# A hybrid mixer block on one core: the output gates' stage in the rounds' pools, and longer transfer estimates for the planner

## The chip, the cores and the metric

The program runs on one core of one Trainium2 chip. A core has a tensor engine (PE, whose weight loads are shown apart as PEld), a vector engine (DVE), a scalar engine (ACT), GpSimd (POOL), and SyncE (SP), which issues every transfer of this program from one queue. The metric is the device time of one execution in microseconds.

## The reference, cut to what matters

One layer over 256 context tokens and 2048 latent tokens of width 1024, in float32. A modulated norm and one wide input projection `z` come first; its columns go to four mixers, each with four heads and a forward and a backward scan over chunks of 64 tokens. The sum of the two scans is normalised by head and multiplied by an output gate that is also a part of `z`. An output projection, a squared-ReLU MLP and a last norm follow.

```python
z = (jnp.concatenate([hc, hx], axis=1) @ w_in[layer]).astype(jnp.float32)
z_ml, z_rw, z_gl, z_gd = _split(z, (ML_W, RW_W, GL_W, GD_W))
mixed = jnp.concatenate([_mlstm_mixer(z_ml, ...), _rwkv_mixer(z_rw, ...), _gla_mixer(z_gl, ...), _gdn_mixer(z_gd, ...)], -1)
x = x + gate1_x * (mixed[:, n_ctx:] @ w_out[layer])
x = x + gate2_x * _mlp(_rms(x, norm2_w[layer]) * (1 + scale2_x) + shift2_x, mlp_w1[layer], mlp_w2[layer])
return _rms(x, final_norm_w)
# in a mixer:
y_fwd = scan_fn(*fwd_args)
y_bwd = scan_fn(*[_rev(t, n_ctx) for t in bwd_args])
y = _head_rms(y_fwd + _rev(y_bwd, n_ctx), norm_w) * jax.nn.sigmoid(o)          # mLSTM; GLA and GDN gate with silu
# in the RWKV-7 and GDN scans, for each chunk:
sol = lax.linalg.triangular_solve(m, rhs, left_side=True, lower=True, unit_diagonal=True)
```

## The kernel before

The 36 chunks of 64 tokens are worked through in six parts (`CHUNKS`), in five **rounds** (round 0 takes the context and one latent part, the rounds 1 to 4 one part each). Each round normalises its tokens (`make_h`: POOL multiplies `xh` by the row norm `rbr`, ACT scales it and rounds it to `hh`, DVE leaves the rest in `hl`), multiplies them with the columns of `w_in` (PE tiles `ps_z`, each operand as a rounded part and a rest, so three products for one), and stores what the scans need in DRAM (`x_fm`, `x_tm`, `x_rows`, `x_bg`). `hh` and `hl` are one buffer each, so a round's first `ps_z` waits for the last `ps_z` of the round before.

Beside the projections run two streams that mostly wait for each other and for transfers:

- **Solves** (`solve`): the triangular systems of up to four units (a direction and two chunks). For each unit `solve_prep` loads `s_s_b` and `s_s_x`, makes products `ps_n` and stores a matrix to `x_sN`; `find` loads them together into `s_s_b`, inverts 32x32 blocks in 31 steps of two instructions (`s_t`, `s_s_x`; on POOL for the rounds 0 to 3, on DVE for round 4) and stores `x_sX`; then `solve_post` loads that for each unit, makes products `ps_s` and stores `x_t`. The tiles `s_s_b` and `s_s_x` have one buffer each, so units follow one another.
- **Groups** (`group`): one chunk of one direction. It loads `ff`, `kc`, `rw`, `t` and `tm`, makes products `ps_att`, `ps_ml`, `ps_R`, `ps_U` and `ps_S`, writes the next state `St`, and makes the outputs `ps_ym` and `ps_ylgr`, which are left in `yall`. The first of a chunk's two directions stores `yall` to `x_gat`; the **second** loads what the first left (the 512 columns `yp`) and the gates (640 columns `gat`), adds, runs `finish` (norm by head, gates on POOL), transposes (`ps_yT`) and stores to `x_mix`.

After round 4 comes the stage of the **output gates** (`out_gates`, called four times): `make_h` again, then for each of three column pairs `tm_tiles` multiplies (two `ps_z` tiles a pair) and a gate tile is put together in a `t4` tile and stored to `x_gat`. Sixteen groups run beside it. The **tail** then works on four blocks of 512 tokens: output projection (`ps_o`), MLP (`ps_f`, `ps_a`), last norm, with the other 24 groups beside it.

Memory is held in **pools**: `phase_pools` opens a set for a stage, and a tile of a new stage waits for the tiles of the old one whose memory it takes. In a pool a tag has a number of buffers; an allocation beyond it waits for the oldest to be read for the last time. The rounds share one set, prefix "r", the gate stage has a set "g", the tail a set "t".

The code is written as generators that `interleave` steps through. The order that the chip sees is made afterwards by a **planner** in the framework (`schedule_with_timeline_sim=True`): it simulates the program with a table of costs and writes out, for each engine, a list in the order in which its simulation started things. On the chip each engine runs its list in that order and waits where an input isn't there. A transfer's estimated length in this table thus decides how much other work the planner lists before the transfer's first reader.

Of the kernel before, what the change touches and what calls it, by code (L numbers as in the profile page):

```python
# [4 lines left out]

# [5 lines left out]

F32 = mybir.dt.float32
F32R = mybir.dt.float32r
# [37 lines left out]
GC = 1  # L51
# [124 lines left out]
class Kern:  # L176
# [1262 lines left out]
    def wt(self, nm, shape, bufs=None):  # L1439
        return self.wp.tile([128] + shape, F32, tag=nm, name=nm, bufs=bufs or 2)  # L1440

    def by_half(self, t, src):

        for h, p in enumerate(SL):
            self.dma(t[p], src[:, h])

    def group(self, d, c0):
        X, R, sl = self.X, range, SL
# [49 lines left out]
        for ft in R(2):  # L1498
            x, n = (2 * ft, 2) if hasq else (1 + ft, 1)
# [89 lines left out]
        new = self.state[d] = self.state_tile()  # L1589
# [11 lines left out]

        yall = self.lt("yall", [GC, 4, 128])
        if second:
            gat = self.lt("gat", [GC, 1152])
            self.by_half(gat[:, 0], X["gat"][c0])
            yp, gat = gat[:, :, 0:512].rearrange("p c (m f) -> p c m f", m=4), gat[:, :, 512:]
        for ms in ("m", "lgr"):
            b = self.bank(self.qa, "yy", "ps_y" + ms, 1)
            first, then, last = [], [], []
            for mi, mm in enumerate(ms):  # L1610
                w = 65 if mm == "m" else 64
                for ft, p in fp:
                    y = slice(128 * mi + w * ft, 128 * mi + w * ft + w)
                    f, c, t, v = {"m": (Lq[:, 2 + ft], cm(ft), Lt[:, 6 + ft], vm(ft)), "l": (ff[:, 4 + ft], cl(ft), lS[:, ft], vl(ft)),
                                  "g": (Lq[:, ft], f2[ft], Lt[:, 4 + ft], U[:, g2[ft]]),
                                  "r": (ff[:, 3 * ft], cr(ft), Lt[:, 3 * ft], vr(ft))}[mm]
# [21 lines left out]
        if not second:  # L1638
            for h, p in enumerate(sl):
                self.dma(X["gat"][c0, :, h, 0:512], yw[p, 0])  # L1640
        else:
            self.finish(yall, gat)
            b = self.psum("ps_yT", "yt" if "yt" in self.pb else "pp")
            for m in R(4):
                self.tr(b[:, 128 * m:128 * m + 128], yall[:, 0, m])
            yT = self.lt("sq", [512])
            self.act(yT, b, AF.Copy)
            self.dma(X["mix"][:, c0].rearrange("p m r t -> p (m r t)"), yT)
            self.done.add(c0)

    def finish(self, yall, gat):

        nh = 8 * GC
        bc = [128, nh, 64]
        sq = self.lt("sq", [512]).rearrange("p (n d) -> p n d", d=64)
        ss, rs = self.wt("ss", [nh]), self.wt("rs", [nh])
        y = yall.rearrange("p c m (f d) -> p (c m f) d", f=2)
        v = lambda t: t.rearrange("p (c m f) -> p c m f", c=GC, m=4)

        s1 = self.wt("s1", [GC, 2])  # L1660
        yr = yall[:, :, 3].rearrange("p c (f d) -> p c f d", f=2)
        self.V.reduce_sum(s1, yr, axis=AX.X)
        self.stt(yr, s1.unsqueeze(3).to_broadcast([128, GC, 2, 64]), -1.0 / 64, yr, ALU.mult, ALU.add)
        self.act(sq, y, AF.Square)
        self.V.reduce_sum(ss, sq, axis=AX.X)

        self.ts(v(ss)[:, :, 3], v(ss)[:, :, 3], 64 * (GN_EPS - EPS), ALU.add)
        self.ts(ss, ss, 1.0 / 64, ALU.mult, EPS, ALU.add)
        self.inv_sqrt(rs, ss, self.wt("rqt", [nh]))
        self.tt(y, y, rs.unsqueeze(2).to_broadcast(bc), ALU.mult)  # L1670
        self.tt(yall[:, :, 0:3], yall[:, :, 0:3], gat[:, :, 0:384].rearrange("p c (m f) -> p c m f", m=3), ALU.mult, e=self.G)
        gr = gat[:, :, 384:640].rearrange("p c (f x d) -> p c f x d", f=2, x=2)
        self.tt(yr, yr, gr[:, :, :, 0], ALU.mult, e=self.G)
        self.tt(yr, yr, gr[:, :, :, 1], ALU.add, e=self.G)
# [137 lines left out]
def body(ctx, tc, A, out):  # L1812
    K = Kern(ctx, tc, A, out)
# [7 lines left out]
    def groups(d, cs):  # L1821
        return [lambda c=c: K.group(d, c) for c in cs]
    down = lambda a, b: range(a, b - 1, -1)
    def mix(a, b):

        n = max(len(a), len(b))
        o = []
        for i in range(n):
            o += a[len(a) * i // n:len(a) * (i + 1) // n] + b[len(b) * i // n:len(b) * (i + 1) // n]
        return o  # L1830
# [13 lines left out]
    with ExitStack() as both:  # L1844
        K.sp = both.enter_context(tc.tile_pool(name="sp", bufs=1))
        with ExitStack() as es:
# [8 lines left out]
            c = [(0, K.cond(0, "s_b", 1))]  # L1855
# [17 lines left out]
                solves([(B, 24), (F, 18), (B, 22), (F, 20)], [(B, 20), (F, 22), (B, 18), (F, 24)], [(B, 6), (B, 4)], beside=True)  # L1873
                finals((F, 2), (F, 1), (B, 3))
            interleave(K.round_(4, r4), q, groups(F, range(10, 18)), 29, 0.1)
        with ExitStack() as es:
            K.phase_pools(es, "g", {"": 4, "gat": 2, "yall": 2, "sq": 1}, {"pp": 2, "pc": 1})
            gap = mix(groups(F, range(18, 24)), groups(B, down(25, 16)))
            interleave(chain(K.out_gates(5, 1), K.out_gates(4), K.out_gates(3), K.out_gates(2)), q, gap, 24, 0.1)
    with ExitStack() as es:  # L1880
        K.tail_pools(es)
        blocks = [[(16, 8)], [(8, 8)], [(24, 8)], [(4, 4), (32, 4)]]
        interleave(K.tails(blocks), q, mix(groups(B, down(15, 8)), groups(F, range(24, 32)))
                   + mix(groups(B, down(7, 4)), groups(F, range(32, 36))), 296, 0.0, 0.35)


# [13 lines left out]
```

## Time and profile before

| | us |
|---|---|
| median of the runs | 4298.56 (4298.08 to 4305.28, 3 runs) |
| the profiled execution, its own time | 4309.05 |
| its span | 4307.2 |
| PE busy in the span | 3517.9 (82%) |
| DVE / ACT / POOL busy | 2464.7 / 1399.0 / 1451.0 |
| rounds 0 to 4, about | 0 to 1970 |
| output gates' stage, about | 1970 to 2380 |
| tail, about | 2380 to 4307 |

The stages are told apart by their tiles: the first `gate` tile is written at 1989.3 and the last at 2357.4; the groups' last transfer of `gat` is issued at 3212.3. In a window's row the busy time of each engine stands with its instruction count, then the granted clock of PE as a share of full speed, the mean busy share of the DMA engines and their rate. A row of a list of waits reads: who waited, on which line, for whom, microseconds in total, times, the longest. In a timeline row the brackets hold the idle time just before and what ended it. Lines L184, L188, L192, L197, L200, L228 and L239 are helpers (`tt`, `ts`, `stt`, `act`, `dma`, `weave`, `mm`), so tiles tell more than lines.

### The profile page before, as it was taken

The page shows a single profiled execution, that of the slowest core. Times are in us where ns is not written, and L with a number is a line of the kernel's source. Part 1 is how long each engine was busy: PE and PEld are TensorE (multiplying, and loading weights), DVE is VectorE, ACT ScalarE, POOL GpSimd, SP SyncE. Part 2 cuts the span into 40 slices and gives each one's busy share as a digit, 9 for nine tenths or more (in the row PEclk, how much of TensorE's full clock was granted, in tenths as well). Part 3 has the DMA queues.
Part 4 walks back from the last instruction along what each step waited for, and adds up shares of the span by engine and source line. Part 5 has one row for each costly group of instructions (what it writes and reads, how often), then busy time and mean ns, then how long its engine had stood idle before and what let it go on. Part 6 is the DMA issues. An engine that isn't in the chain of part 4 may idle for free. (4 is left out here: it accounts for less than half of the span.)

```text
span 4307.2 us, 75017 instructions
## 1 busy us (share of the span) xinstructions
PE 3517.9 (82%) x29082; PEld 2847.4 (66%) x29082; DVE 2464.7 (57%) x5259; ACT 1399.0 (32%) x2544; POOL 1451.0 (34%) x1682
## 2 busy tenths in 40 slices
PE   6356777776777767666888799999999999999998
PEld 5245556555655656555777577777778778877886
DVE  7653765566476548646665465666764454445444
ACT  3224432442333233333423232223323332233322
POOL 3212553544153253512224323334432242224222
PEclk9667876887887787667888899999999999999999
DMA  6566466746766665667764644546442324232322
GB/s 215 121 135 130 109 164 148 166 109 145 161 145 127 141 158 125 147 149 188 203 180 140 183 128 145 149 138 172 134 150 96 104 90 134 93 103 84 112 98 83
DMA packets 609092, 592.66 MB, mean 138 GB/s; under 512 B 286128, under 2 KB 486912, under 8 KB 608736
## 3 DMA queue, kind: packets, MB, share of 16 engines
q1 hardware_dynamic: 608736, 587.87, 51.8%
q8 instruction: 229, 3.75, 0.4%
q14 instruction: 127, 1.04, 0.1%
HBM read 463.78 MB, written 123.92 MB: 136 GB/s over the span
## 5 line engine op out<-in xcount | busy, mean ns | idle before, releaser
L184 POOL TENSOR_TENSOR w_lo<-w_f,w_hi 128x1024 fp32r<-128x1024 f32 x213 | 513.9, 2413 | 1180.8 <-ACT w_hi L197 1119.4
L197 ACT ACTIVATE w_hi<-w_f 128x1024 fp32r<-128x1024 f32 (+1 forms) x427 | 448.6, 1051 | 910.8 <-PE ps_a L239 375.8
L239 PE MATMUL ps_a<-ah,w_hi 128*128 128x512 f32 x1024 | 407.7, 403 | 6.1 <-ACT ah L197 6.1
L239 PE MATMUL ps_f<-h2l,w_hi 128*128 128x512 f32 x1024 | 404.1, 396 | 9.1 <-DVE h2l L192 9.1
L239 PE MATMUL ps_f<-h2h,w_hi 128*128 128x512 f32 x1024 | 404.3, 395 | 2.9 <-ACT w_hi L197 2.7
L239 PE MATMUL ps_a<-al,w_hi 128*128 128x512 f32 x1024 | 406.3, 397 | 0.2 <-DVE al L184 0.2
L239 PE MATMUL ps_f<-h2h,w_lo 128*128 128x512 f32 x1024 | 404.8, 396 | 1.8 <-DVE w_lo L184 1.1
L239 PE MATMUL ps_a<-ah,w_lo 128*128 128x512 f32 x1024 | 400.0, 398 | 0.0
L184 DVE TENSOR_TENSOR w_lo<-w_f,w_hi 128x1024 fp32r<-128x1024 f32 (+1 forms) x214 | 267.9, 1252 | 220.7 <-ACT w_hi L197 218.1
L239 PE MATMUL ps_z<-hh,w_hi 128*128 128x512 f32 (+3 forms) x760 | 306.8, 410 | 48.1 <-ACT hh L197 18.9
L239 PE MATMUL ps_z<-hh,w_lo 128*128 128x512 f32 (+3 forms) x760 | 305.9, 403 | 29.2 <-DVE w_lo L184 22.8
L192 DVE SCALAR_TENSOR_TENSOR x1T<-ps_a,modv,x1T 128x512 f32<-128x512 f32 x256 | 187.7, 748 | 246.7 <-PE ps_a L239 246.2
L239 PE MATMUL ps_z<-hl,w_hi 128*128 128x512 f32 (+3 forms) x760 | 305.3, 402 | 8.5 <-DVE hl L184 8.1
L184 DVE TENSOR_TENSOR relu<-relu 128x512 f32<-128x512 f32 x128 | 188.0, 1470 | 110.1 <-ACT relu L197 110.1
L239 PEld LDWEIGHTS ps_a<-ah,w_hi 128*128 128x128 f32 x1024 | 191.1, 188 | 62.5 <-ACT ah L197 14.7
L211 PE MATMUL ps_z<-w_hi,hh 128*128 128x256 f32 x672 | 213.6, 319 | 20.5 <-ACT hh L197 11.5
L239 PEld LDWEIGHTS ps_f<-h2l,w_hi 128*128 128x128 f32 x1024 | 194.4, 190 | 52.0 <-DVE h2l L192 10.3
L239 PEld LDWEIGHTS ps_f<-h2h,w_hi 128*128 128x128 f32 x1024 | 194.2, 190 | 45.9 <-ACT w_hi L197 4.4
L239 PEld LDWEIGHTS ps_f<-h2h,w_lo 128*128 128x128 f32 x1024 | 194.4, 190 | 44.4 <-DVE w_lo L184 1.9
L239 PEld LDWEIGHTS ps_a<-ah,w_lo 128*128 128x128 f32 x1024 | 193.0, 189 | 45.6 <-issue 0.5
L239 PEld LDWEIGHTS ps_a<-al,w_hi 128*128 128x128 f32 x1024 | 193.3, 189 | 44.3 <-DVE al L184 0.5
L239 PEld LDWEIGHTS ps_z<-hh,w_hi 128*128 128x128 f32 (+1 forms) x760 | 160.3, 213 | 87.4 <-ACT hh L197 22.4
(428 smaller groups left out, 8022.7 us busy)
## 6 DMA issues: line engine op xcount, KB each, us to landing
w_f<-w SPq DMA_DIRECT2D x256, 512.0 KB
w_f<-wg SPq DMA_DIRECT2D x90, 512.0 KB
tm<-x_tm SPq DMA_DIRECT2D x144, 259.5 KB
kc<-x_fm SPq DMA_DIRECT2D x64, 448.0 KB
adaw<-ada SPq DMA_DIRECT2D x48, 512.0 KB
rw<-x_rows SPq DMA_DIRECT2D x144, 160.0 KB
w_f<-wp SPq DMA_DIRECT2D x44, 512.0 KB
gat<-x_gat SPq DMA_DIRECT2D x64, 288.0 KB
```

The costliest lines, as they stand in the source:

```text
L184: return (e or self.V).tensor_tensor(out=o, in0=a, in1=b, op=op)
L192: return self.V.scalar_tensor_tensor(o, a, s, b, op0, op1)
L197: return self.S.activation(o, a, f, bias=bias, scale=scale)
L211: i = self.T.matmul(o, l, r, start=k == 0, stop=k == len(mms) - 1)
L239: return self.T.matmul(o, l, r, start=start, stop=stop)
```

## The change

Two things change.

**Pools.** The set "g" goes. The calls of `out_gates` and their 16 groups run inside the rounds' set, which stays open. There the tags of a group's loads `kc`, `rw`, `t` and of `Lt`, `Lq` have 2 buffers (4 in "g"), `ff` and `tm` 3 (4 in "g"), `yall` 1 (2 in "g"). The rounds' set has no tags `gat` and `sq`, so a second group of this stage takes the tile for `yp` from the tag `a5` (of the projections, 4 buffers), the one for `gat` from `z5` (of the projections, 2 buffers), and `sq` from `cv` (2 buffers); the half-rows of 1152 numbers are loaded as 512 and 640, in four transfers where there were two. The tail's groups load as before. The gate tiles' `t4` is now the same tag `x4`, with 2 buffers, that round 4's second solve uses.

**Estimates.** While the program is planned, three costs of the planner's table are other: the fixed issue cost of an SP transfer is 825 ns (625 in the framework's table), its start delay 1400 ns (650), and the rate of one of the 16 DMA engines 16 bytes/ns (22.5). They are numbers of the planner, not of the chip: no transfer is changed by them. For 128 KB the planner's price rises by 0.20 + 0.75 + 0.15 = 1.10 us, for 512 KB by 1.56 us.

```diff
+    def sq_tile(self):
+        if "sq" in self.lb:
+            return self.lt("sq", [512])
+        return self.pp.tile([128, 512], F32, tag="cv", name="sq", bufs=2)
...
         if second:
-            gat = self.lt("gat", [GC, 1152])
-            self.by_half(gat[:, 0], X["gat"][c0])
-            yp, gat = gat[:, :, 0:512].rearrange("p c (m f) -> p c m f", m=4), gat[:, :, 512:]
+            if "gat" in self.lb:
+                gat = self.lt("gat", [1152])
+                self.by_half(gat, X["gat"][c0])
+                yp, gat = gat[:, 0:512], gat[:, 512:1152]
+            else:
+
+                yp, gat = self.pp.tile([128, 512], F32, tag="a5", name="yp", bufs=4), self.z5("gat")[:, 0:640]
+                self.by_half(yp, X["gat"][c0, :, :, 0:512])
+                self.by_half(gat, X["gat"][c0, :, :, 512:1152])
...
-            yT = self.lt("sq", [512])
+            yT = self.sq_tile()
...
-        sq = self.lt("sq", [512]).rearrange("p (n d) -> p n d", d=64)
+        sq = self.sq_tile().rearrange("p (n d) -> p n d", d=64)
...
             interleave(K.round_(4, r4), q, groups(F, range(10, 18)), 29, 0.1)
-        with ExitStack() as es:
-            K.phase_pools(es, "g", {"": 4, "gat": 2, "yall": 2, "sq": 1}, {"pp": 2, "pc": 1})
             gap = mix(groups(F, range(18, 24)), groups(B, down(25, 16)))
             interleave(chain(K.out_gates(5, 1), K.out_gates(4), K.out_gates(3), K.out_gates(2)), q, gap, 24, 0.1)
...
+@contextmanager
+def transfers():
+
+    SP = mybir.EngineType.SP
+    new = {"HWDGE_FIXED_OVERHEAD_NS": {**TRN2Spec.HWDGE_FIXED_OVERHEAD_NS, SP: 825},
+           "DGE_DMA_DELAY": {**TRN2Spec.DGE_DMA_DELAY, SP: 1400},
+           "DMA_BUS_BYTES_PER_NS_PER_ENGINE": 16.0}
+    old = {k: getattr(TRN2Spec, k) for k in new}
+    for k, v in new.items():
+        setattr(TRN2Spec, k, v)
+    try:
+        yield
+    finally:
+        for k, v in old.items():
+            setattr(TRN2Spec, k, v)
...
-    with tile.TileContext(nc, schedule_with_timeline_sim=True) as tc:
+    with transfers(), tile.TileContext(nc, schedule_with_timeline_sim=True) as tc:
```

The planner makes another order of it from round 1 on. Three places are shown; numbers behind names are those of tiles, and the lines of the changed file are one higher.

**First place: PE at the end of round 4.** `ps_z_18288` is the last projection tile of round 4. Before, solve products and groups follow it; the first pair of gate tiles comes 79 rows later, behind the output of the last group of this round:

```order
L211 MATMUL ps_z_18288<-w_hi_18284,hh_14451 128x256
L211 MATMUL ps_z_18288<-w_lo_18286,hh_14451 128x256
L211 MATMUL ps_z_18288<-w_hi_18284,hl_14452 128x256
L239 MATMUL ps_s_17092<-s_s_b_17079 32x32 x16
L239 MATMUL ps_s_17092<-s_s_x_17080 32x32 x16
L247 MATMUL ps_tm_18154<-pack_58,lx_18140 128x128 x2
L228 MATMUL ps_ym_17328<-St_16691,Lq_17226 64x65 x4
```

```order
L228 MATMUL ps_ylgr_18540<-tm_18420,glS01_225 64x64 x4
L228 MATMUL ps_ylgr_18540<-U_18496,Lt_18423 64x64 x4
L228 MATMUL ps_ylgr_18540<-tm_18420,Lt_18423 64x64 x4
L228 MATMUL ps_ylgr_18540<-U_18496,ara_18439 64x64 x4
L211 MATMUL ps_z_18662<-w_hi_18652,hh_18592 128x256
L211 MATMUL ps_z_18662<-w_lo_18654,hh_18592 128x256
L211 MATMUL ps_z_18711<-w_hi_18652,hh_18592 128x256
```

Now the first pair (`ps_z_18645` and `ps_z_18694`) stands right behind it, and the products that stood there come after the pair, beginning with `ps_s` of round 3's last solve (`ps_s_16545`, three units earlier than the `ps_s_17092` above):

```order
L212 MATMUL ps_z_18288<-w_hi_18284,hh_14451 128x256
L212 MATMUL ps_z_18288<-w_lo_18286,hh_14451 128x256
L212 MATMUL ps_z_18288<-w_hi_18284,hl_14452 128x256
L212 MATMUL ps_z_18645<-w_hi_18635,hh_18575 128x256
L212 MATMUL ps_z_18645<-w_lo_18637,hh_18575 128x256
L212 MATMUL ps_z_18694<-w_hi_18635,hh_18575 128x256
L212 MATMUL ps_z_18694<-w_lo_18637,hh_18575 128x256
L212 MATMUL ps_z_18645<-w_hi_18635,hl_18576 128x256
```

```order
L212 MATMUL ps_z_18694<-w_hi_18641,hh_18575 128x256
L212 MATMUL ps_z_18694<-w_lo_18643,hh_18575 128x256
L212 MATMUL ps_z_18694<-w_hi_18641,hl_18576 128x256
L247 MATMUL ps_col_23235<-pack_58,mf_m_23220 64x32 x2
L247 MATMUL ps_col_23590<-pack_58,mf_bi_23574 64x16 x2
L240 MATMUL ps_s_16545<-s_s_b_16532 32x32 x16
L247 MATMUL ps_col_23590<-pack_58,mf_ee_23576 64x16 x2
L240 MATMUL ps_s_16545<-s_s_x_16533 32x32 x16
L229 MATMUL ps_ym_16698<-St_16307,Lq_16596 64x65 x4
```

The pair has moved ahead of a stretch of solves and groups, and the stretch has grown: 131 rows now stand between this pair and the next gate tile. Counted in products, `ps_s_16545` is number 7428 on PE before and number 7576 now, with the pair's 96 products and four of `ps_col` among those that have come ahead of it.

**Second place: POOL, the preparation of the first gate tiles.** Before, the eight multiplications of `xh` stand together behind the clearing of `s_s_x` for round 4's first solve:

```order
L1301 MEMSET s_s_x 128x1024
L1302 MEMSET s_s_x 128x32
L184 TENSOR_TENSOR St<-St,reg 128x128
L184 TENSOR_TENSOR xh<-xh,rbr 128x512 x8
L184 TENSOR_TENSOR St<-St,rw 128x128
L184 TENSOR_TENSOR St<-St,reg 128x128
```

Now they stand inside the inversion of round 3's last solve:

```order
L185 TENSOR_TENSOR s_t<-s_s_b,s_s_x 128x207
L185 TENSOR_TENSOR xh<-xh,rbr 128x512
L185 TENSOR_TENSOR s_s_x<-s_s_x,s_t 128x9x23
L185 TENSOR_TENSOR xh<-xh,rbr 128x512
L185 TENSOR_TENSOR s_t<-s_s_b,s_s_x 128x192
L185 TENSOR_TENSOR xh<-xh,rbr 128x512
L185 TENSOR_TENSOR s_s_x<-s_s_x,s_t 128x8x24
L185 TENSOR_TENSOR xh<-xh,rbr 128x512
L185 TENSOR_TENSOR s_t<-s_s_b,s_s_x 128x175
L185 TENSOR_TENSOR s_s_x<-s_s_x,s_t 128x7x25
L185 TENSOR_TENSOR xh<-xh,rbr 128x512
L185 TENSOR_TENSOR s_t<-s_s_b,s_s_x 128x156
```

**Third place: PE in a solve of round 3.** `ps_n_13696` belongs to one unit of that solve and reads what was loaded into `s_s_b`. Before:

```order
L228 MATMUL ps_R_14349<-St_14076,ff_14290 64x64 x4
L228 MATMUL ps_R_14349<-St_14076,kw_14325 64x64 x3
L239 MATMUL ps_ml_14338<-kc_14291 64x128
L239 MATMUL ps_a_13155<-wa_11613,rwup_262 128x256
L239 MATMUL ps_ml_14338<-kc_14291 64x128
L228 MATMUL ps_R_14349<-St_14076,kw_14325 64x64
L239 MATMUL ps_n_13696<-s_s_b_13686 64x64 x16
L239 MATMUL ps_ml_14338<-kc_14291 32x128 x2
```

Now projection products of round 4 (`hh_14451`) stand ahead of the same product, where before small products of a group and of the RWKV part stood:

```order
L240 MATMUL ps_z_15124<-hl_14452,w_hi_15120 128x256
L240 MATMUL ps_z_15124<-hh_14451,w_lo_15122 128x256
L240 MATMUL ps_z_15124<-hh_14451,w_hi_15120 128x256
L240 MATMUL ps_z_15124<-hl_14452,w_hi_15120 128x256
L240 MATMUL ps_z_15124<-hh_14451,w_lo_15122 128x256
L240 MATMUL ps_n_13696<-s_s_b_13686 64x64 x16
L240 MATMUL ps_ml_14338<-kc_14291 64x128 x2
L229 MATMUL ps_R_14349<-tm_14299,Lt_14302 64x64 x4
```

The solves and groups of the rounds 2 to 4 have moved back against the projections. From the second pair of gate tiles on, the groups stand at nearly the same number on PE as before.

More of the change, by code (lines that the diff above doesn't have):

```diff
@@ L2 @@
 import math
-from contextlib import ExitStack
+from contextlib import ExitStack, contextmanager
 from itertools import chain
@@ L10 @@
 from concourse import mybir
+from concourse.hw_specs import TRN2Spec
 F32 = mybir.dt.float32
@@ L1603, in group @@
         if second:
-            gat = self.lt("gat", [GC, 1152])
-            self.by_half(gat[:, 0], X["gat"][c0])
-            yp, gat = gat[:, :, 0:512].rearrange("p c (m f) -> p c m f", m=4), gat[:, :, 512:]
+            if "gat" in self.lb:
[6 more added lines that the diff above has]
+                self.by_half(gat, X["gat"][c0, :, :, 512:1152])
+            yp, gat = yp.rearrange("p (c m f) -> p c m f", c=GC, m=4), gat.rearrange("p (c f) -> p c f", c=GC)
         for ms in ("m", "lgr"):
```

## The prediction

> **What bounds the kernel now.** I first read the page's forty slices: from slice 23 on PE is busy nine tenths or more of nearly each, before it five to eight. The windows by stage say it in numbers (busy us and instructions of PE, PEld, DVE, ACT, POOL; granted clock; DMA share; GB/s):
>
> ```profile
> 400.00:1890.00 1490.00, 1075.63 (x10648) 862.88 (x10646) 911.06 (x2145) 544.73 (x1120) 637.77 (x987) 0.77 0.62 143
> 1890.00:1970.00 80.00, 35.16 (x675) 32.37 (x676) 37.09 (x113) 10.69 (x28) 6.82 (x10) 0.63 0.52 121
> ...
> 2000.00:2380.00 380.00, 313.29 (x4780) 280.14 (x4780) 232.58 (x664) 129.73 (x279) 112.62 (x122) 0.84 0.68 185
> 2380.00:2400.00 20.00, 5.19 (x55) 4.04 (x52) 4.76 (x12) 3.28 (x6) 3.50 (x4) 0.59 0.35 107
> 2400.00:4307.00 1907.00, 1847.39 (x11614) 1468.19 (x11612) 1020.53 (x1630) 585.10 (x848) 582.79 (x378) 0.99 0.39 121
> ```
>
> In the last row PE is busy 97%: the tail is bounded by PE, and a microsecond won ahead of it is won at the end. Before it nothing is full. In the rounds PE idles 1490 - 1076 = 414 us, DVE 579 us. At the end of round 4 (1890 to 1970) PE works 35 of 80 us; in the gates' stage 82% again. So the rounds are bounded by in-order lists that wait for one another, and I ask who waits there. PE's eleven largest rows, 400 to 1890:
>
> ```profile
> PE ps_s L239 <- ACT s_s_b L197: 43.4, 17, 8.7
> PE ps_ml L239 <- DVE Lt L184: 31.1, 15, 5.9
> PE ps_rb L247 <- ACT rb L197: 30.2, 15, 6.8
> PE ps_R L228 <- DVE Lt L184: 29.6, 8, 13.3
> PE ps_ke L247 <- DVE ke L184: 29.1, 14, 6.4
> PE ps_n L239 <- DMA s_s_b<-x_fm: 27.8, 12, 8.7
> PE ps_ylgr L228 <- DVE yall L184: 23.1, 10, 6.2
> PE ps_z L239 <- ACT hh L197: 18.9, 7, 6.4
> PE ps_tm L247 <- DVE lx L184: 17.7, 3, 12.2
> PE ps_s L239 <- DMA s_s_b<-x_sN: 12.2, 6, 4.7
> PE ps_ss L239 <- DVE cv L184: 8.9, 4, 3.6
> ```
>
> The two rows of `ps_s` and those of `ps_ml`, `ps_R`, `ps_n` and `ps_ylgr` are steps of solves and groups, 167 of the 272 us of the eleven rows (61%); the other five belong to the projections' own work. DVE's transfer rows of the same stretch tell what feeds those six:
>
> ```profile
> DVE s_s_b L184 <- DMA s_s_x<-x_bg: 56.8, 14, 10.0
> DVE ga L184 <- DMA tm<-x_tm: 50.9, 14, 7.7
> ...
> DVE s_s_x L1383 <- DMA s_s_b<-x_sX: 40.7, 11, 9.9
> ...
> DVE kw L184 <- DMA kc<-x_fm: 21.6, 9, 4.3
> ...
> DVE kw L184 <- DMA rw<-x_rows: 17.2, 9, 3.7
> DVE s_s_b L1378 <- DMA s_s_b<-x_sX: 16.4, 7, 4.2
> ```
>
> **Term 1, the estimates in the rounds.** These are 64 waits of DVE and, with the two transfer rows of PE, 82 waits of 244 us, 3.0 us each. The list had put the reader that much too early. The new table makes the planner think of a 128 KB transfer as 1.10 us longer, so it lists that much more work ahead of each reader; the third place of the order shows it, with products of `ps_z` where small ones stood. If each wait shrinks by 1.10 us, that is 90 us of engine time. Not all of it reaches the end, since an engine may have waited for another thing at once; I take the share that the solves and groups have in PE's rows, 0.61: **-55 us**. Bounds: 0 (the work put ahead is only moved) and -114 us (the four PE rows that a late transfer can stand behind vanish: 43.4 + 31.1 + 27.8 + 12.2). The same transfers also end waits of ACT and POOL; I don't count them twice.
>
> Does a transfer need the longer estimate? A small one:
>
> ```profile
> 1929.65 0.60 SPq L200 DMA_DIRECT2D gc<-x_tm  x1
> 1932.03 0.42 DVE L184 TENSOR_TENSOR s_x<-gc,s_x 128x256 f32<-128x256 f32 x1 [4.72 <-DMA gc<-x_tm]
> 1939.83 2.01 SPq L200 DMA_DIRECT2D s_s_b<-x_sN  x2
> 1945.48 0.19 DVE L184 TENSOR_TENSOR s_t<-s_s_b,s_s_x 128x31 f32<-128x31 f32 x1 [6.85 <-DMA s_s_b<-x_sN]
> ```
>
> `gc`, a few KB, is read 2.4 us after its issue began. The second of the two loads of `x_sN` is issued at about 1940.8 and read 4.6 us later. [...] The Trainium skill (DMA: Bandwidth & Descriptors, Specifications) puts the first-byte latency of the hardware-generated path at about 0.6 us. By that rule the table's old 650 ns of delay was right, 1400 ns moves readers back for nothing, and the time would be that of the first rival; no row here separates the first byte from the landing.
>
> **Term 2, the first pair of gate tiles.** Before, its loads stand in SP's list behind the last solve units, since the set "g" takes the memory of the rounds' set:
>
> ```profile
> 1966.19 11.07 POOL L184 TENSOR_TENSOR xh<-xh,rbr 128x512 f32<-128x512 f32 x8 [24.69 <-DMA xh<-xT]
> 1969.32 0.58 PE L211 MATMUL ps_z<-w_hi,hh 128*128 128x256 f32 x1 [4.30 <-ACT hh L197]
> ...
> 1985.03 0.29 PE L211 MATMUL ps_z<-w_hi,hl 128*128 128x256 f32 x1
> ...
> 1988.99 0.40 PE L211 MATMUL ps_z<-w_hi,hl 128*128 128x256 f32 x2
> ```
>
> From POOL's first multiplication at 1966.2 to the pair's end at about 1990, 24 us go by in which PE has little but the pair. Now the pair stands ahead of the solves. The next gate tiles can follow the stretch at once, and the gates' stage, 82% PE, starts that much further on. What covers PE there now is the second pair; round 4's inversion on DVE goes on until 1985 and would otherwise be waited for. I take 0.82 of 24: **-20 us**; bounds 0 (the inversion and its `solve_post` are waited for) and -24.
>
> **Term 3, what the pair is put ahead of.** The solve chain (one buffer each of `s_s_b` and `s_s_x`) must run to the end before the gates' groups can use its result. Its step `ps_s_16545` comes 148 products later, 100 of them the pair and four `ps_col`. The other 48, two records each at 1490/10648 = 0.14 us, are 13 us. The pair's 96 products run at 0.12 us each when nothing is missing (33 rows in 3.96 us, from 1985.03 to 1988.99): 11.5 us. Together **+25 us**. Bounds: +13 (the pair lies wholly behind the inversion on POOL) and +36 (the eight multiplications, 11.07 us, also lengthen that inversion).
>
> **Term 4, fewer buffers beside the gates.** Two buffers of `kc`, `rw`, `t` in place of four cost nothing as long as a group's loads, some 5 us, fit into the 380/16 = 24 us between groups; without that cover each would be late by its transfer. A single `yall` is held from its first write to the last transpose:
>
> ```profile
> 2367.12 0.29 DVE L184 TENSOR_TENSOR yall<-ps_ym,dn 128x128 f32<-128x128 f32 x1
> ...
> 2378.18 0.29 DVE L184 TENSOR_TENSOR yall<-ps_ym,dn 128x128 f32<-128x128 f32 x1
> 2379.15 0.47 PE L247 MATMUL ps_yT<-pack,yall 128*128 128x128 f32 x1
> ```
>
> The next group's first write, at 2378.2 here, must wait until 2379.6. That is 1.4 us, and behind it on DVE wait the next state updates. Eight second groups: **+11 us**; bounds 0 and +50 (half of each 12.5 us hold). Sixteen more transfer issues of some 0.5 us lie in SP's free time; without that cover they are 8 us. The hole at 2380 (PE 5 of 20 us) stays: the tail's set still takes the memory of the set before it, so 0.
>
> The sum is -55 - 20 + 25 + 11 = **-39 us**. The profiled execution would take 4309.05 - 39 = 4270, the runs, 10.5 us lower, 4298.56 - 39.
>
> **The rivals.**
>
> - *The wait moves, it doesn't shrink.* The work listed ahead of a reader is taken from later; the solves, which are a chain, fall behind the projections, and at the end of round 4 nothing is left to cover them but one pair of tiles. The place is the stretch between the pair and the second gate tile, 131 rows where 79 stood. It decides if term 1 is under about 16 us. For it: PE already works only 35 of 80 us there. Against: most waits of the table above end with a transfer, not with a chain. The price is term 1: 4260 + 55 = **4315**, slower.
> - *More than the estimate's share.* With projection products ahead of them, the four PE rows of 114 us vanish whole: 4260 - 60 = **4200**. For it: a projection tile is many times longer than 1.1 us. Against: projections run out at each round's end.
> - *The gates' stage pays for its buffers.* Each of eight second groups is held up for half of `yall`'s 12.5 us, +50 in place of +11: 4260 + 39 = **4299**, no change. For it: groups of both directions alternate. Against: 24 us lie between groups on average.
>
> That the order stays as it was can be left out: the three places show that it moved.
>
> **How the numbers follow.** My forecast has 0.52, the first rival 0.22, the second 0.16, the third 0.10. About 0.2% (8.6 us) is what can be told from no change. The forecast, own range 4225 to 4292, gives 0.46 faster, 0.02 same, 0.04 slower; the first rival 0.17 slower, 0.05 same; the second 0.16 faster; the third 0.02 faster, 0.05 same, 0.03 slower. Together faster 0.64, same 0.12, slower 0.24. The time is 4260. Eight times in ten should lie between 4185, below the second rival, and 4330, above the first.
>
> **What would show it.** Term 1: the six DVE transfer rows from 400 to the end of round 4 add up to some 90 us less, and PE's idle time of the rounds falls from 414 to about 360. Term 2: the first `gate` tile is written before the last `ps_n` of round 4's first solve, not after it. Term 3: between the first and the second pair PE has a hole, longer than today's 80 us by some 25. Term 4: `yall` appears in DVE's waits for `ps_yT`. The tail's windows should keep their length, 1907 us from its start; if the tail gains or loses over 15 us, the forecast is wrong in a place that I did not look for, and if the rounds' waits are as large as before, the first rival is right.

## The result and the profile after

The changed kernel takes **4180.06 us** (median of 4 runs, 4172.70 to 4181.71); the kernel before beside it 4298.32 (4292.56 to 4305.28). The ratio is 0.9721 (95% interval 0.9702 to 0.9739): 118 us less, where 39 were predicted. The time lies 5 us below the lower end of the range.

The span fell by 127.3 us, from 4307.2 to 4179.9. The gate tiles come in four sets, one for each call of `out_gates`, of three pairs each. The windows below are cut at the writes of `hh`: start of round 1, of round 4, of the first set of gate tiles, of the second set, of the last set. Where an expectation below measures up to the second pair of gate tiles, its numbers are those up to the second set. A row gives busy us and instructions of PE, PEld, DVE, ACT, POOL; granted clock; DMA share; GB/s. Before:

```profile
445.36:1590.46 1145.10, 856.34 (x8174) 673.74 (x8174) 700.14 (x1610) 404.48 (x807) 494.45 (x746) 0.78 0.62 142
1590.46:1968.65 378.19, 239.73 (x3044) 210.13 (x3044) 228.32 (x609) 127.25 (x298) 124.13 (x211) 0.69 0.58 140
1968.65:2040.96 72.31, 54.87 (x548) 50.53 (x548) 43.36 (x110) 28.26 (x58) 20.00 (x17) 0.81 0.81 218
2040.96:2263.43 222.47, 183.17 (x2952) 164.09 (x2952) 148.46 (x425) 78.87 (x172) 55.94 (x67) 0.84 0.74 193
```

The changed kernel, at the same writes:

```profile
404.24:1424.24 1020.00, 786.36 (x7504) 619.78 (x7505) 689.91 (x1537) 399.02 (x783) 492.31 (x735) 0.81 0.71 153
1424.24:1750.59 326.35, 217.79 (x2620) 189.00 (x2618) 220.40 (x562) 113.27 (x260) 143.77 (x226) 0.73 0.64 153
1750.59:1939.79 189.20, 117.81 (x1704) 104.58 (x1704) 79.41 (x240) 54.84 (x127) 34.97 (x51) 0.69 0.56 143
1939.79:2132.10 192.31, 170.51 (x2848) 153.42 (x2850) 142.71 (x411) 76.09 (x162) 56.66 (x65) 0.88 0.78 213
```

| stretch | before | after | difference |
|---|---|---|---|
| up to the start of round 4 | 1590.5 | 1424.2 | -166.2 |
| start of round 4 to the second set of gate tiles | 450.5 | 515.6 | +65.1 |
| second set to the last set of gate tiles | 222.5 | 192.3 | -30.2 |
| from there to the end | 2043.8 | 2047.8 | +4.0 |

Up to round 4 each round takes some 41 us less than it took (the starts are earlier by 41, 83, 127 and 166 us). Part of that is only work put off: PE does 670 products fewer in the rounds 1 to 3 (7504 where 8174 stood), and 732 more from the start of round 4 to the second set (2620 + 1704 against 3044 + 548). A product here is a record of the profile; a small float32 product has two of them. A good third of the rounds' gain is given back there.

There is a second way to split the 127 us. PE idles 71.5 us less (717.8 for 789.3), and PE is *busy* 55.8 us less (3462.1 for 3517.9), with the same 29082 products.

**The waits.** DVE's waits for transfers, changed kernel, 400 to 1750 (its first gate tiles), the rows that answer to the six of the prediction:

```profile
DVE s_s_b L185 <- DMA s_s_x<-x_bg: 24.6, 6, 9.3
...
DVE kw L185 <- DMA rw<-x_rows: 14.0, 4, 5.1
DVE s_s_x L1384 <- DMA s_s_b<-x_sX: 13.9, 2, 8.4
...
DVE ga L185 <- DMA tm<-x_tm: 12.1, 8, 2.2
...
DVE kw L185 <- DMA kc<-x_fm: 8.9, 3, 3.6
...
DVE s_s_b L1379 <- DMA s_s_b<-x_sX: 4.0, 4, 2.0
```

They were 64 waits of 203.6 us, 3.2 each; they are 27 waits of 77.5 us, 2.9 each. The counts alone don't tell how: an equal 2.5 us off each of the 64 would leave 32 waits of 81 us. Following the readers does (the same instruction, counted by its place among those of its kind): 38 of the 64 no longer wait for a transfer at all, 16 of them out of the 25 that had waited over 3 us, and several of the 26 that are left wait longer than before. So most waits went whole instead of shrinking a little. PE's rows in the same window:

```profile
PE ps_ke L248 <- DVE ke L185: 63.7, 18, 8.5
PE ps_z L240 <- ACT hh L198: 34.2, 8, 11.6
...
PE ps_ml L240 <- DVE Lt L185: 10.6, 7, 5.6
...
PE ps_s L240 <- DMA s_s_b<-x_sN: 8.1, 3, 6.7
...
PE ps_s L240 <- ACT s_s_b L198: 5.5, 7, 2.1
...
PE ps_n L240 <- DMA s_s_b<-x_fm: 4.8, 2, 2.9
```

The four rows that a late transfer can stand behind fell from 114 to 29 us. The largest are now `ps_ke` (29 us before, 64 now) and `ps_z` behind `hh`: steps of the projections' own work.

**The solves.** They did not gain what the projections gained. Before, the store of round 3's last inversion, just behind its last step on POOL:

```profile
1817.98 0.40 SPq L200 DMA_DIRECT2D x_sX<-s_s_x  x1
```

The same store in the changed kernel, then the first gate tile, a `ps_n` behind it (of a unit of round 4, since round 3's inversions are over), and the start of round 4's inversion on DVE:

```profile
1769.43 0.44 SPq L201 DMA_DIRECT2D x_sX<-s_s_x  x1
...
1772.32 0.60 ACT L198 ACTIVATE gate<-ps_z 128x512 f32<-128x512 f32 x1 [4.51 <-PE ps_z L212]
...
1847.53 1.15 PE L240 MATMUL ps_n<-s_s_b 64*64 64x64 f32 x32 [1.82 <-ACT yall L198]
...
1884.02 0.19 DVE L185 TENSOR_TENSOR s_t<-s_s_b,s_s_x 128x31 f32<-128x31 f32 x1 [3.09 <-DMA s_s_b<-x_sN]
```

Round 3's inversion ends 49 us earlier and round 4's begins 61 us earlier (1945.5 before), while the projections of round 4 began 166 us earlier. The gates' first pair now stands ahead of the solves, and then PE has little until the solves come: the first pair ends at 1775.3 and the second begins at 1899.4, and in these 124 us PE is busy for 61. Before, the second pair followed the first within 1 us.

### The profile page after: what moved, and what is told of

Its sections match the earlier page's. It is cut to its first block, busy times and chain, and to the rows that moved or that the text cites. A ratio compares the mean times of both kernels' runs of the same rounds, so it can differ in the third digit from the quotient of the medians.

```text
span 4179.9 us, 75082 instructions
## 1 busy us (share of the span) xinstructions
PE 3462.1 (83%) x29082; PEld 2807.3 (67%) x29082; DVE 2490.3 (60%) x5259; ACT 1403.3 (34%) x2544; POOL 1464.4 (35%) x1682
## 4 chain that ended last, share of the span: by engine, by line
PE 42%; DVE 4%; issue 1%; POOL 1%; ACT 1%; DMA 1%; SPq 0%; POOLq 0%; DVEq 0%; ACTq 0%
PE ps_a L240 17%; PE ps_f L240 15%; PE ps_o L240 4%; PE ps_ylgr L229 1%; PE ps_z L212 1%; PE ps_S L229 1%; PE ps_att L240 1%; DVE h2l L193 1%; DVE relu L185 1%; PE ps_R L229 1%; SPq L201 0%; PE ps_ym L229 0%; PE ps_yT L248 0%; PE ps_ml L240 0%; POOL yall L185 0%
```

## The experiments

All times are medians; the interval is that of the ratio to the kernel before on the same chip. "Estimates" are issue cost, start delay, rate.

| run | pools | estimates | us | ratio (95%) |
|---|---|---|---|---|
| changed kernel | new | 825, 1400, 16 | 4180.06 | 0.9721 (0.9702 to 0.9739) |
| e1 | old | 825, 1400, 16 | 4212.05 | 0.9800 (0.9781 to 0.9819) |
| e2 | new | 625, 650, 22.5 | 4321.17 | 1.0057 (1.0039 to 1.0076) |
| e3 | new | 625, 1400, 22.5 | 4251.92 | 0.9894 (0.9876 to 0.9911) |
| e4 | new | 625, 650, 16 | 4243.22 | 0.9869 (0.9841 to 0.9896) |
| e5 | new | 725, 1025, 19 | 4212.41 | 0.9818 (0.9792 to 0.9843) |
| e6 | new | 1025, 2150, 12 | 4316.72 | 1.0060 (1.0044 to 1.0077) |
| e7 | new | 825, 1300, 16 | 4137.64 | 0.9641 (0.9623 to 0.9659) |
| e8 | old, fewer buffers | 825, 1400, 16 | 4205.56 | 0.9805 (0.9786 to 0.9824) |
| e9 | new | 825, 1200, 16 | 4174.61 | 0.9709 (0.9689 to 0.9730) |
| e10 | new | 825, 1500, 16 | 4157.24 | 0.9676 (0.9662 to 0.9691) |
| e11 | old | 825, 1300, 16 | 4189.66 | 0.9750 (0.9734 to 0.9766) |
| e12 | old | 625, 700, 22.5 | 4278.52 | 0.9949 (0.9930 to 0.9967) |

### One part alone

The estimates without the pools (e1, against the kernel before):

```diff
+@contextmanager
+def transfers():
+    new = {"HWDGE_FIXED_OVERHEAD_NS": {**TRN2Spec.HWDGE_FIXED_OVERHEAD_NS, SP: 825},
+           "DGE_DMA_DELAY": {**TRN2Spec.DGE_DMA_DELAY, SP: 1400},
+           "DMA_BUS_BYTES_PER_NS_PER_ENGINE": 16.0}
...
-    with tile.TileContext(nc, schedule_with_timeline_sim=True) as tc:
+    with transfers(), tile.TileContext(nc, schedule_with_timeline_sim=True) as tc:
```

> The pools stay as before; only the three transfer estimates change. Theory E (the estimates carry the gain, in the rounds): the starts of the rounds 1 to 4 come some 40 us apart earlier each, as in the changed kernel (334 to 350 us a round where 376 to 389 stood), and the time is 4170 to 4230. Theory P (the pools carry it: the first gate pair fills the hole and no set of pools is closed): the rounds keep 376 to 389 us and the time is 4270 to 4300.

The pools without the estimates (e2, against the changed kernel):

```diff
-    with transfers(), tile.TileContext(nc, schedule_with_timeline_sim=True) as tc:
+    with tile.TileContext(nc, schedule_with_timeline_sim=True) as tc:
```

> The pools change, the estimates stay at 625 ns, 650 ns and 22.5 bytes/ns. Theory E: rounds of 376 to 389 us as before, and a time of 4270 to 4310 (my terms 2 to 4 together gave +16 with bounds on both sides). Theory P: 4180 to 4230. Theory L (any other order of this planner moves the time by tens of us, whatever the reason): anything from 4200 to 4400, with rounds that differ from 376 to 389 by over 10 us although no estimate changed.

Theory E holds for the first: -84 us, within its 4170 to 4230, and the rounds 1 to 4 begin at 401.8, 735.6, 1074.2 and 1429.5, as in the changed kernel. The pools alone **cost** 25 us, and their rounds begin within 10 us of those before (444.7, 816.9, 1195.1, 1581.1). So the rounds' gain belongs to the estimates. But the parts don't add up: with the estimates the same pools win 32 us. By stage, old pools with the estimates (e1), from round 4 on, cut as above:

```profile
1429.46:1876.84 447.38, 274.56 (x3750) 239.27 (x3746) 258.72 (x690) 136.68 (x323) 158.91 (x259) 0.69 0.59 139
1876.84:1948.97 72.13, 52.93 (x476) 47.88 (x476) 41.59 (x98) 26.08 (x46) 22.98 (x18) 0.82 0.82 222
1948.97:2160.55 211.58, 173.52 (x3040) 157.57 (x3040) 152.03 (x445) 81.65 (x184) 52.72 (x65) 0.87 0.79 203
```

From the start of round 4 to the second set it takes 519.5 us, the changed kernel 515.6: with the first pair ahead of the solves, the new pools win 4 us there. From the second set to the last it takes 211.6, in the changed kernel 192.3: 19 us.

### Which of the numbers

Two of the three numbers put back, with the new pools. The start delay alone (e3):

```diff
-    new = {"HWDGE_FIXED_OVERHEAD_NS": {**TRN2Spec.HWDGE_FIXED_OVERHEAD_NS, SP: 825},
+    new = {"HWDGE_FIXED_OVERHEAD_NS": {**TRN2Spec.HWDGE_FIXED_OVERHEAD_NS, SP: 625},
            "DGE_DMA_DELAY": {**TRN2Spec.DGE_DMA_DELAY, SP: 1400},
-           "DMA_BUS_BYTES_PER_NS_PER_ENGINE": 16.0}
+           "DMA_BUS_BYTES_PER_NS_PER_ENGINE": 22.5}
```

> The new pools, and of the estimates only the start delay, 1400 ns in place of 650: 0.75 of the 1.10 us that a 128 KB transfer is thought longer. Theory E: 0.68 of the estimates' gain; if the estimates alone give 110 us and the pools nothing, 4298 - 75 = about 4223. Theory L: no relation to the share; it could lie above 4298.

The rate alone (e4):

```diff
-    new = {"HWDGE_FIXED_OVERHEAD_NS": {**TRN2Spec.HWDGE_FIXED_OVERHEAD_NS, SP: 825},
+    new = {"HWDGE_FIXED_OVERHEAD_NS": {**TRN2Spec.HWDGE_FIXED_OVERHEAD_NS, SP: 625},
-           "DGE_DMA_DELAY": {**TRN2Spec.DGE_DMA_DELAY, SP: 1400},
+           "DGE_DMA_DELAY": {**TRN2Spec.DGE_DMA_DELAY, SP: 650},
            "DMA_BUS_BYTES_PER_NS_PER_ENGINE": 16.0}
```

> The new pools, and of the estimates only the rate, 16 bytes/ns in place of 22.5 for one of 16 DMA engines: 0.15 of the 1.10 us for 128 KB. Theory E: 0.14 of the gain, so about 4283, less than with the delay alone. Theory L: no relation to the share. If the planner's picture of a busy queue rests on the rate more than on the delay (a theory Q), the rate alone gives more than the delay alone: under 4220.

Against the same pools without estimates (4321.17), the delay alone wins 69 us and the rate alone 78; their intervals overlap, so neither is shown to win more. Theory E had 4223 for the delay and 4283 for the rate, and missed both. I had the rate at a fifth of the delay's weight, 0.15 against 0.75 us for 128 KB. All DVE waits ended by a transfer, summed from the start to round 4, say the same: 320 us without estimates, 246 with the delay, 213 with the rate, 141 with all. Theory Q is right that the rate weighs more than a lone transfer's length says; its bound, under 4220, was not reached. That the planner's queue of transfers is what multiplies the rate is argued, not shown.

### How far it goes

Half the step (e5):

```diff
-    new = {"HWDGE_FIXED_OVERHEAD_NS": {**TRN2Spec.HWDGE_FIXED_OVERHEAD_NS, SP: 825},
+    new = {"HWDGE_FIXED_OVERHEAD_NS": {**TRN2Spec.HWDGE_FIXED_OVERHEAD_NS, SP: 725},
-           "DGE_DMA_DELAY": {**TRN2Spec.DGE_DMA_DELAY, SP: 1400},
+           "DGE_DMA_DELAY": {**TRN2Spec.DGE_DMA_DELAY, SP: 1025},
-           "DMA_BUS_BYTES_PER_NS_PER_ENGINE": 16.0}
+           "DMA_BUS_BYTES_PER_NS_PER_ENGINE": 19.0}
```

> The new pools, with each estimate half-way: 725 ns, 1025 ns, 19 bytes/ns. With none of the estimates these pools took 4321.17 us, with all of them 4180.06. Theory E (each reader is moved back by the estimate's share, and the wait shrinks by it): between the two, near 4250 (4225 to 4275). Theory L (luck of one order): outside 4180 to 4321, or within 10 us of either end.

A second step of the same size (e6):

```diff
-    new = {"HWDGE_FIXED_OVERHEAD_NS": {**TRN2Spec.HWDGE_FIXED_OVERHEAD_NS, SP: 825},
+    new = {"HWDGE_FIXED_OVERHEAD_NS": {**TRN2Spec.HWDGE_FIXED_OVERHEAD_NS, SP: 1025},
-           "DGE_DMA_DELAY": {**TRN2Spec.DGE_DMA_DELAY, SP: 1400},
+           "DGE_DMA_DELAY": {**TRN2Spec.DGE_DMA_DELAY, SP: 2150},
-           "DMA_BUS_BYTES_PER_NS_PER_ENGINE": 16.0}
+           "DMA_BUS_BYTES_PER_NS_PER_ENGINE": 12.0}
```

> The new pools, with each estimate as much longer again: 1025 ns, 2150 ns, 12 bytes/ns. Theory E in its simple form (a longer estimate always covers more): 4100 to 4160. Theory M (the gain ends where the estimate meets the chip's own transfer: 143 GB/s at a busy share of 0.62 is 231 GB/s, or 14.4 bytes/ns for one of 16 engines, which 16 nearly reaches and 12 passes): 4170 to 4230, no better than the changed kernel, since readers are then listed later than their data, and the rounds lengthen again.

Steps of 100 ns in the start delay (e7; with 1200 e9, with 1500 e10):

```diff
     new = {"HWDGE_FIXED_OVERHEAD_NS": {**TRN2Spec.HWDGE_FIXED_OVERHEAD_NS, SP: 825},
-           "DGE_DMA_DELAY": {**TRN2Spec.DGE_DMA_DELAY, SP: 1400},
+           "DGE_DMA_DELAY": {**TRN2Spec.DGE_DMA_DELAY, SP: 1300},
            "DMA_BUS_BYTES_PER_NS_PER_ENGINE": 16.0}
```

> The changed kernel with a start delay of 1300 ns in place of 1400, 0.1 of 1.1 us less for 128 KB; a control of what a small step in a number does through another order. Theory E: 4180 to 4195, rounds within 10 us of 334 to 350. Theory L: off by 30 us or more in either direction.

> The changed kernel with a start delay of 1200 ns. Theory B (the time is the sum of two things that move in steps with the estimate: waits for transfers that vanish, and solves that fall behind): DVE's waits for transfers up to round 4 lie between those of the half-way estimates (207 us) and of 1300 ns (128 us), and the time between 4138 and 4212, near 4160. Theory L (luck of an order, on top of the trend): the waits as said, but the time off 4160 by 30 us or more.

> The changed kernel with a start delay of 1500 ns. Theory B: fewer waits of DVE for transfers (under 141 us up to round 4), more given back from the start of round 4 to the second pair of gate tiles (over the 516 us of the changed kernel), and a time of 4190 to 4230. Theory L: under 4170 or over 4250, with the same waits.

With the new pools (the sum of waits is that of DVE for transfers up to round 4, and in brackets all its idle time there):

| estimates | us | waits | start of round 4 | from there to the second set |
|---|---|---|---|---|
| framework's | 4321.17 | 320 (609) | 1581 | 447 |
| half | 4212.41 | 207 (514) | 1501 | 437 |
| delay 1200 | 4174.61 | 135 (488) | 1469 | 454 |
| delay 1300 | 4137.64 | 128 (470) | 1453 | 453 |
| delay 1400, the change | 4180.06 | 141 (470) | 1424 | 516 |
| delay 1500 | 4157.24 | 152 (452) | 1448 | 466 |
| a second step | 4316.72 | 44 (531) | 1477 | 579 |

Three things follow. The gain isn't one lucky order: it rises from nothing over the half step (which came out faster than the 4225 to 4275 of theory E) to a plateau, and four orders on the plateau take 4138 to 4180. It ends: with a second step DVE's waits for transfers are nearly gone, and the time is that of the framework's numbers. Other waits have come in their place, among them PE's for the loads of `ps_n`; of e6, DVE and PE from the start to round 4:

```profile
DVE Lt L185 <- PE ps_att L240: 43.2, 5, 20.3
```

```profile
PE ps_ke L248 <- DVE ke L185: 69.4, 22, 10.8
PE ps_rb L248 <- ACT rb L198: 66.2, 22, 9.8
PE ps_n L240 <- DMA s_s_b<-x_fm: 44.9, 5, 13.6
```

and its solves are far behind: the store of round 3's last inversion is issued at 1865.2, 96 us after the changed kernel's. The stretch from round 4 to the second set is the longest of all, with PE idle for 227 of 579 us:

```profile
1476.54:1867.98 391.44, 241.65 (x3392) 209.99 (x3392) 236.64 (x640) 125.36 (x296) 149.17 (x256) 0.73 0.58 143
1867.98:2055.15 187.17, 110.00 (x1700) 99.31 (x1700) 80.81 (x233) 53.49 (x126) 28.08 (x33) 0.69 0.57 145
```

This is the first rival, at an estimate twice as far. The simple form of theory E, that longer always covers more, falls; theory M named the size, 4170 to 4230, wrongly.

Third, on the plateau 100 ns of one number move the time by some 20 to 40 us, without order: e7 was expected within 15 us and came out 42 faster (34 by the ratios), e10 was expected slower and came out 23 faster. Both theories of a smooth sum failed there (e9 did come out where theory B had it, between 4138 and 4212). This isn't the measurement: two of these kernels, run again later, came out at 4171.27 (4174.61) and 4155.91 (4157.24). The changed kernel is the fastest of them up to round 4 and loses most after it. In e10 the store of round 3's last inversion and the start of round 4's come 44 and 28 us before the changed kernel's 1769.43 and 1884.02:

```profile
1725.87 0.34 SPq L201 DMA_DIRECT2D x_sX<-s_s_x  x1
...
1856.33 0.19 DVE L185 TENSOR_TENSOR s_t<-s_s_b,s_s_x 128x31 f32<-128x31 f32 x1 [4.84 <-DMA s_s_b<-x_sN]
```

A small step at the other end, the kernel before with a start delay that is 50 ns longer (e12; the framework's numbers stand in the rows taken out):

```diff
     new = {"HWDGE_FIXED_OVERHEAD_NS": {**TRN2Spec.HWDGE_FIXED_OVERHEAD_NS, SP: 625},
-           "DGE_DMA_DELAY": {**TRN2Spec.DGE_DMA_DELAY, SP: 650},
+           "DGE_DMA_DELAY": {**TRN2Spec.DGE_DMA_DELAY, SP: 700},
            "DMA_BUS_BYTES_PER_NS_PER_ENGINE": 22.5}
```

> The kernel before, with a start delay of 700 ns in place of 650 and nothing else; a control of what another order alone does at that end. Theory B: 4285 to 4300, and rounds within 5 us of 376 to 389. Theory L: off by 30 us or more.

It won 18 us, between the two theories; its round 4 begins at 1554 in place of 1590, and 12 us of that are lost by the second set.

### The buffers, and the pools with other estimates

The estimates with the old pools, the gates' own set cut to the rounds' numbers (e8):

```diff
-            K.phase_pools(es, "g", {"": 4, "gat": 2, "yall": 2, "sq": 1}, {"pp": 2, "pc": 1})
+            K.phase_pools(es, "g", {"ff": 3, "tm": 3, "gat": 2, "yall": 1, "sq": 1}, {"pp": 2, "pc": 1})
```

> The estimates alone (4212.05 us), and in the gates' stage's own set of pools the numbers of buffers that the rounds' set has: kc, rw, t, Lt, Lq 2 in place of 4, ff and tm 3, yall 1 in place of 2. Nothing of the rounds changes. My term 4 (the single yall and fewer loads ahead cost 11 us, bounds 0 and 50): 4212 + 11 = 4223, up to 4262. If the 25 us that the pools cost without the estimates come from the shared tags a5, z5, cv and x4 and not from these numbers: within 5 us of 4212.

4205.56, ratio 0.9805 beside 0.9800: the numbers of buffers cost nothing that can be told. In the changed kernel the single `yall` shows only this in DVE's waits for the transposes from the second set to the last:

```profile
DVE yall L185 <- PE ps_yT L248: 3.3, 2, 1.6
```

Two waits, 3.3 us together, where I had taken eight of 1.4.

The old pools at other estimates (the kernel of e1 with 1300, the half step, 1200 and 1500):

> The pools as before, with the estimates 825 ns, 1300 ns and 16 bytes/ns. With 1400 ns the new pools were worth 32 us (4212.05 to 4180.06), without the estimates they cost 25. If that worth belongs to the estimates' size: 4138 + 32 = 4170, between 4155 and 4185. If it is one order's luck: outside that.

> Old pools, estimates half-way (with the new pools 4212.41 us). Theory I (interplay: with the old set the solves that the estimates push back must be through before the first gate tile, with the new one they run beside the gates; so the pools' worth grows with what is pushed back): here half-way between -25 and +42, so about 4220 (4205 to 4235). Theory L (luck of each order): outside 4180 to 4250 or on the other side of 4212 by more than 15.

> Old pools, start delay 1200 ns (with the new pools 4174.61 us). Theory I: slower by 30 to 50, so 4205 to 4225; the stretch from the start of round 4 to the second gate tile's pair 5 to 20 us longer than the 454 us with the new pools, and the gates' stage 20 to 35 longer than 208. Theory L: under 4195.

> Old pools, start delay 1500 ns (with the new pools 4157.24 us). Theory I: 4187 to 4210, with the gates' stage 20 to 35 us longer than 198. Theory L: under 4177.

e11 took 4189.66 us, 52 more than with the new pools, just past what was expected of one fixed worth. The other three took 4157.04, 4162.68 and 4146.59 (ratios 0.9814, 0.9820, 0.9793), but on a chip on which the kernel before took 4236.83: compared by their ratios the pools would be worth nothing at the half step, 1.1% at 1200 and 1.2% at 1500, but a chip with faster transfers also changes what an estimate is worth. So one pair was run again on one chip, and one kernel beside it:

> New pools, start delay 1200 ns, beside the old pools on the same chip. Theory I (interplay): faster than the old pools of the next run by 30 to 60 us. Theory C (the difference of the last pairs was the chips'): within 15 us of it.

> Old pools, start delay 1200 ns, the other half of this pair. Theory I: a ratio to the kernel before of 0.978 to 0.984, and the run above at 0.968 to 0.975. Theory C: both within 0.004 of each other.

> New pools, start delay 1500 ns. If this chip's kernel before takes about 4237 us, Theory I: 30 to 60 us under the 4146.59 us of the old pools there, so 4087 to 4117; Theory C: 4130 to 4160. If it takes about 4297, a repeat of 4157 within 10 us under both.

The chip was of the slower kind (before 4296.89). New pools 4171.27 (0.9712, 0.9693 to 0.9731), old 4200.44 (0.9776, 0.9761 to 0.9791), and 4155.91 for 1500 (0.9674, 0.9655 to 0.9694). The pair differs by 29 us, one below theory I's 30 to 60 and well over theory C's 15. Where it differs, from round 4 on, new pools:

```profile
1461.66:1918.76 457.10, 295.72 (x3818) 261.89 (x3814) 278.56 (x737) 157.34 (x365) 169.50 (x270) 0.73 0.62 154
1918.76:2123.37 204.61, 170.93 (x2844) 155.00 (x2840) 149.13 (x426) 74.93 (x167) 57.17 (x64) 0.88 0.74 201
```

and old pools:

```profile
1458.64:1933.36 474.72, 291.74 (x3612) 257.23 (x3606) 276.53 (x708) 153.50 (x343) 172.79 (x267) 0.72 0.61 148
1933.36:2165.27 231.91, 183.87 (x3053) 165.15 (x3055) 158.44 (x464) 83.05 (x188) 62.89 (x72) 0.84 0.74 192
```

By the second set the new pools have done 206 products more in 18 us less, and from there to the last set they are 27 us shorter. So with estimates from 1200 on the new pools won in all three pairs of chips of one kind, 29, 52 and 32 us (27, 47 and 34 by the ratios; only the first pair ran on one chip); without them they cost 25. This is what the interplay says; that what wins is the pushed-back solves running beside the gates is argued from the places, and since single orders scatter by some 20 us, how the worth grows with the estimate stays open, as does the cost of 25 us at the old estimates (its profiled run is 9 us over the one before: 9 less up to round 4, 4 less to the second set, 6 more to the last set and 16 more after it).

**A version that beats both** came out of it: the changed kernel with a start delay of 1300 ns, 4137.64 us, 0.9641 of the kernel before.

## Why the prediction was wrong

**What bounds the kernel** was read rightly: the rounds' in-order lists, with DVE's and PE's waits behind transfers, and a tail that keeps its length (2044 and 2048 us from the last set of gate tiles).

**Two steps failed: term 1 itself, and adding the pools' terms to it.** The sum missed 79 us. With the estimates put in first, they gave -84 where -55 stood, about 29 us of the miss, and the pools then gave -32 where +16 stood, about 48.

**Term 1 (-55)** failed in three ways. Its price of a transfer, 1.10 us for 128 KB alone, gave the rate 0.15 us of it, and the rate alone took 107 us out of DVE's transfer waits up to round 4, where the delay took 74. Its form, each wait shrinks by the price, was wrong: most waits go whole, 64 become 27, and the six rows lost 126 us where I wrote "some 90" (PE's idle time from 400 to the end of round 4 fell from 414 to 344, where I wrote 360). This was the second rival's mechanism, which took 85 of its 114 us. Its time, 4200, was the nearest of the four, but partly by luck: it counted idle time alone, as my sum did. The estimates alone brought the profiled span from 4307.2 to 4213.7: PE's idle time fell by 40.2 us, a little *less* than my 55, and its busy time by 53.3, which the sum put at nothing without a reason.

That busy time is the granted clock. The record of it in the traces is full or half at any moment. Laid over PE's busy time, it shows 732.5 us of work under the half clock before, 643.2 with the estimates alone and 632.7 in the changed kernel. Over all 20 profiles, a microsecond less of busy time under the half clock goes with 0.52 us less busy time in all (correlation 0.98). One tile shows the two speeds (minimum, median, maximum in ns). Before, with the estimates alone (e1), and with the second step (e6):

```profile
L239 PE MATMUL ps_n<-s_s_b x1024: 218/267/366, 350.9 to 2129.7; 64*64 64x64 f32 x171
```

```profile
L240 PE MATMUL ps_n<-s_s_b x1024: 216/218/367, 357.7 to 2048.8; 64*64 64x64 f32 x171
```

```profile
L240 PE MATMUL ps_n<-s_s_b x1024: 216/311/367, 436.4 to 2164.7; 64*64 64x64 f32 x171
```

The median of those that start under the full clock is 218 in all three, under the half clock 311, and 498, 447 and 532 of the 1024 start under the half clock. The three medians thus jump because about half of the products are slow, and this tile alone says little of the sum: in e6 it is slower than before, yet PE is busy for 3472.2 us, 46 less than before. What e6 loses is idle time, 57 us more than before.

The granted clock of the rounds 1 to 3 is 0.78 before and 0.81 in the changed kernel. The Trainium skill (TensorE: Matmul & The Clock Gate, Part 1: The HAM clock gate) says that the clock follows how busy the array has lately been, and halves after an idle stretch; the trace agrees in the two speeds and in the direction. Its remark that the ramp is under 1% of a typical span is no guide to this kernel, which before was busy under the half clock for 732.5 of 4307.2 us. The reading of the first byte's latency that I had set against term 1 would have made the longer delay worthless; the delay alone won 69 us, so nothing of that is seen.

**The first rival** was right about the place and wrong about the sign of the whole: 65 of the 166 us won by round 4 are lost up to the second set, more than any other order of the plateau loses; but the rounds won far more than the 16 us that I had made its condition.

**Terms 2 and 3 (-20, +25).** The pair stands where I said (first gate tile at 1772.3, round 4's `ps_n` after it), and between the first two pairs is the hole that I said, 124 us with PE idle for 63, where I wrote 80 + 25 and 80 with 45 idle stood ahead of the pair. I priced it by the chain's lag of 148 products, and that count was wrong: number 7428 before is the next unit's product, `ps_s_16796`; `ps_s_16545` is number 7304 there, so it comes 272 products later. In the traces the first product of `ps_s_16545`, at 1825.8 before and 1777.7 now, has 11162 records of PE ahead of it before and 11450 now. That is 288 more, 96 of them the pair and 144 other `ps_z`. With the pair at the prediction's 11.5 us and the other 192 at its 0.14, they are 38 us, not 25. The chain really lagged 166 - 61 = 105 us behind round 4's start, but that came from the estimates, for e1 with the old pools took as long (519.5 against 515.6). What the pools themselves do there with the estimates is -4 us in that stretch and -19 from the second set to the last.

**Term 4 (+11)** is nothing, and with it the third rival's +50: e8 stands at 0.9805 beside 0.9800.

The pools together, +16 in my sum, came out at +25 without the estimates and at -32 with them. The mistake under it is that I costed the two parts one by one and added them; they change the same order. Why the pools' worth turns with the estimates is not shown.

## What to carry to other kernels

Where a planner writes the order from its own estimates, a latency that was taken too short cost three times here: the wait, everything queued in order behind it, and more of PE's work under the half clock. The estimates are worth a sweep over several steps and past the optimum, in which the waits for transfers should fall and the other waits be watched to rise. Neighbouring orders differ by tens of microseconds that have nothing to do with the idea, so one value proves little, and a change of pools has to be judged at the estimates with which it will run.

## What the runs showed of the hardware

- The same products took 53 us less of PE's time when only the order of the program changed; 89 us less of that time lay under the half clock. One 64x64 product took 218 ns (median) under the full clock and 311 under the half clock, not twice as long.
- The chips aren't alike. The kernel before took 4236.83 us on one of them and 4292 to 4298 on the others. The kernel of e14 and e17 is one and the same. Its packets' share of 16 engines' span was, on the faster chip and on the other,

```profile
q1 hardware_dynamic: 608736, 587.87, 51.4%
```

```profile
q1 hardware_dynamic: 608736, 587.87, 53.0%
```

of spans of 4165.7 and 4199.4 us: 2141 and 2226 us for the same bytes, 4% less on the faster chip. There the estimates with the old pools won 1.8%, on the other 2.2%.
- At a busy share of 0.62 the DMA engines moved 143 GB/s in the rounds before, which is, as an estimate, 231 GB/s at full, or 14.4 bytes/ns for one of 16; over the whole span 47% of the packets are under 512 B (286128 of 609092). The changed table's 16 is nearer to that than 22.5.
